# Retention's decayed queries made on GpSimd by token tile and transposed; group norm in two halves

## The chip, the core and the metric

The kernel runs on one core of one Trainium2 chip. The metric is device time in microseconds (us) of one execution; the median of several is given where there are several. One more execution of each kernel is profiled.

## What is computed

One layer of a diffusion backbone: a modulated RMS norm, one input projection, softmax attention (8 heads, 2 key heads, 64 wide) beside bidirectional retention (8 heads), one output projection, and a dense SwiGLU network. There are 1024 latent tokens and 256 context tokens, the width is 1024, all in float32. The change touches retention and its norm, which the reference gives as:

```python
q_decay = jnp.exp(lg[:, None] * (pos + 1.0))[..., None]
def step(state, qkv):
    qc, kc, vc = qkv
    inner = jnp.einsum('bhid,bhjd->bhij', qc, kc) * decay_mat
    o = jnp.einsum('bhij,bhjd->bhid', inner, vc) + jnp.einsum('bhid,bhde->bhie', qc, state) * q_decay
    state = state * chunk_decay + jnp.einsum('bhjd,bhje->bhde', kc * k_decay, vc)
    return state, o
o = o_f + o_b[:, ::-1]
mu = jnp.mean(o, axis=-1, keepdims=True)
var = jnp.mean(jnp.square(o - mu), axis=-1, keepdims=True)
ret = (o - mu) * lax.rsqrt(var + EPS) * silu(g_r)
```

It is done over chunks of 128 tokens, once forward and once over the reversed sequence, each direction with its own decay per head.

## The kernel before

Everything is one function. After the projections (to about 357 us) comes a stage that weaves three streams, written as Python generators: `attention()` (four head pairs, two halves of the queries, ten key tiles; two scores with an exponential and one weighing per tile), `front(h)` for the coming heads (split, transposes, row maxima), and `retain(r)` for four head pairs `r`, one after the other. `weave` gives each stream a number of steps and always advances the one that is furthest behind; a `yield` ends a step. The planned counts are `N_FR, N_RT, N_AT = 13, 38, 40`. The build then orders each engine's instructions by a timeline that it simulates, so that an instruction may stand earlier on its engine than the program has it; `tc.issue_after(x)` keeps the instructions under it behind `x`. Every engine takes its queue in order, and a matmul that waits holds up all matmuls behind it.

A round of `retain(r)` goes through these steps:

- `ret_load` (L708) loads queries, keys, values and gate of the head pair, in tiles of 128 tokens (`rq`, `rk`, `rv`, `rg`), from the SP queue.
- Ten steps: `decayed(t)` (L737, GpSimd) multiplies a key tile by a decay per token, for two heads and two directions, into `qk2` (named `qk` in rows; three buffers); TensorE makes the state increments (L751), ScalarE copies them to `U` (L754, L756).
- In round 0 `decay_matrices` makes `DT` (L721 to L726), the decay matrix of each head, and `QD` (L730), the queries' decay by position for each head half and direction.
- Four steps: TensorE transposes keys and queries (L768, bank `r`), ScalarE copies them to `kT`, `qT` (L769). After each half of `qT` four products with `QD` (L774) give `q2T`, direction 0 on VectorE, direction 1 on GpSimd. Each takes 64 partitions with 512 elements and may move them to the other 64 partitions.
- The scan `ss` over the chunks (L782, VectorE, 16 dependent links of 128x64), copied to `St` (L787, L789, ScalarE).
- `inner(t)`: the products of `qT` and `kT` (L799), multiplied with `DT` by VectorE to `im` (L802). `outer(t)`: `im` with the values (L811) and `q2T` with `St` (L813) added up in PSUM, copied to `ro` (L815).
- Group norm of the whole head pair, 16 groups of 64 for each of 128 partitions: sum, subtraction (L834 to L836, VectorE), square (L839, ScalarE), sum (L840, L841, VectorE), the power on GpSimd (L843), the product with it on VectorE (L845), the product with the gate on GpSimd (L846), the store to `d_r` (L847).

Beside it attention adds up its exponentials in `acc` (L688), on GpSimd for half of the key tiles or more, and the fronts take row maxima `mx` from PSUM (L596, VectorE). The first transposes of a front are at L587, its query split at L577 and L578, its last transposes at L604 and L605. After the last round `rts.close()` frees retention's memory, and `load_w_out` loads and splits the output weights (L875, L125, L126) beside the last head pair of attention, whose results are normalised at L670. Then `mix_in` and `mix_out` begin.

```python
Q_ENG[d].tensor_tensor(out=q2T[d * HD:(d + 1) * HD, j, bsl].rearrange("p (t n) -> p t n", n=P),
                       in0=qT[jsl, bsl].rearrange("p (t n) -> p t n", n=P),
                       in1=QD[jsl, r, d, :].unsqueeze(1).broadcast_to([HD, 4, P]), op=ALU.mult)
```

Of the kernel before, what the change touches and what calls it, by code (L numbers as in the profile page):

```python
# [107 lines left out]
def hybrid_block(ctx: ExitStack, tc, x, c, cx, c_ctx, w_mod, b_mod, g_pre_mix, g_post_mix,  # L108
# [5 lines left out]
    def f(ap):  # L114
        return ap.bitcast(F32)

    def h3(ap):
        return ap.rearrange("p (h d) -> p h d", d=HD)
# [422 lines left out]
        V.tensor_copy(out=lgd[d * HD:(d + 1) * HD, :], in_=lg[d * HD:(d + 1) * HD, d * HR:(d + 1) * HR])  # L541
    S.activation(out=cd, in_=lgd, func=AF.Exp, scale=float(P))

    lgq = bc.tile([P, 4, 2], F32, name="lgq")
    for j in range(2):
        for d in range(2):
            V.tensor_copy(out=lgq[j * HD:(j + 1) * HD, :, d],
                          in_=lg[j * HD:(j + 1) * HD, d * HR:(d + 1) * HR].rearrange("p (r j) -> p r j", j=2)[:, :, j])

    rawp = ph1.enter_context(tc.tile_pool(name="rawp", bufs=4))  # L550
    wks = ExitStack()
    wk1 = wks.enter_context(tc.tile_pool(name="wk1", bufs=1))
# [4 lines left out]
    late.step(2)  # L557
    wks.close()

    qs2, fr = {}, {}  # L560

    def falloc(first, shape, dt, tag, bufs):
        if first == 1:
# [5 lines left out]
    def front(h):  # L569

        kv = h // 4
        if h % 2 == 0:
            qs2[h // 2] = falloc(h, [P, LT, P], F32, "qs", 1)
            nc.sync.dma_start(out=qs2[h // 2], in_=d_p[0:N_LAT, h * HD:(h + 2) * HD].rearrange("(t p) n -> p t n", p=P))
        q3 = falloc(h, [P, LT, 2 * HD + 2], F32R, "q3", 2)
        qs = qs2[h // 2][:, :, (h % 2) * HD:(h % 2 + 1) * HD]
        S.copy(out=q3[:, :, HD:2 * HD], in_=qs)  # L577
        V.tensor_tensor(out=q3[:, :, 0:HD], in0=qs, in1=f(q3[:, :, HD:2 * HD]), op=ALU.subtract)  # L578
# [12 lines left out]
        nm = small.tile([P, LT], F32, tag="nm", name="nm")  # L591
        for t in range(LT):
            for j, (k0, n) in enumerate(((0, 512), (512, 512), (1024, 256))):
                sb = sbank()
                T.matmul(sb[:, :n], lhsT=t1[:, t * P:(t + 1) * P], rhs=K1[:, kv, k0:k0 + n], start=True, stop=True)  # L595
                V.tensor_reduce(out=mx[:, t, j:j + 1], in_=sb[:, :n], axis=AX.X, op=ALU.max)  # L596
            yield
        V.tensor_reduce(out=nm, in_=mx[:, :, 0:3], axis=AX.X, op=ALU.max, negate=True)
        V.tensor_copy(out=q3[:, :, 2 * HD:2 * HD + 1], in_=nm.unsqueeze(2))
        yield  # L600
        for b in range(2):
            tb = sbank(F32R)
# [6 lines left out]
    SKEW, V_ADDS, V_END, Q_ENG = 4, (2, 4, 6, 8), (2, 4, 6, 7, 8, 9), (V, G)  # L609
    weave((project, 18), (chain(front(0), front(1)), 2 * N_FR))  # L610
    ph1.close()
    ps1.close()
# [101 lines left out]

    DT = rt.tile([P, HR, P], F32, name="DT")

    QD = rt.tile([P, 4, 2, P], F32, name="QD")

    def decay_matrices():
        for h in range(HR):  # L720
            V.tensor_scalar(out=DT[:, h, :], in0=dcs[:, C_DF:C_DF + P], scalar1=lg[:, h:h + 1], scalar2=None, op0=ALU.mult)  # L721
# [2 lines left out]
        for h in range(0, HR, 4):  # L724
            S.activation(out=DT[:, h:h + 4, :], in_=DT[:, h:h + 4, :], func=AF.Exp)
            G.tensor_tensor(out=DT[:, h:h + 4, :], in0=DT[:, h:h + 4, :],  # L726
                            in1=dcs[:, C_M:C_M + P].unsqueeze(1).broadcast_to([P, 4, P]), op=ALU.mult)
        for r in range(4):
            for d in range(2):
                S.activation(out=QD[:, r, d, :], in_=dcs[:, C_PR + d * P:C_PR + (d + 1) * P], func=AF.Exp, scale=lgq[:, r, d:d + 1])  # L730

    def retain(r):
        qn, kn, vn, gn = ret_load(r)

        def decayed(t):
            y = rt.tile([P, 2, 2, HD], F32, tag="qk2", name="qk2", bufs=3)
            G.tensor_tensor(out=y, in0=h3(kn[:, t, :]).unsqueeze(2).broadcast_to([P, 2, 2, HD]),  # L737
                            in1=dk[:, 1, 4 * r:4 * r + 4].rearrange("p (j d) -> p j d", d=2).unsqueeze(3).broadcast_to([P, 2, 2, HD]),
                            op=ALU.mult)
            return y  # L740

# [14 lines left out]
                S.copy(out=U[HD:P, LT + 1 - t], in_=h3(ub[HD:P, 0:P]))  # L756
            yield
        if r == 0:
            decay_matrices()
        qT = rt.tile([P, N_LAT], F32, tag="qT", name="qT")  # L760
        kT = rt.tile([P, N_LAT], F32, tag="kT", name="kT")
        q2T = rt.tile([P, 2, N_LAT], F32, tag="q2T", name="q2T")
        for nat, tr in ((kn, kT), (qn, qT)):
            for b in range(2):
                tb = bank("r")
                bsl = slice(b * 512, (b + 1) * 512)
                for i in range(4):
                    T.transpose(out=tb[:, i * P:(i + 1) * P], in_=nat[:, b * 4 + i, :], identity=ident)  # L768
                S.copy(out=tr[:, bsl], in_=tb)  # L769
                if nat is qn:  # L770
                    for j in range(2):
                        jsl = slice(j * HD, (j + 1) * HD)
                        for d in range(2):
                            Q_ENG[d].tensor_tensor(out=q2T[d * HD:(d + 1) * HD, j, bsl].rearrange("p (t n) -> p t n", n=P),  # L774
                                            in0=qT[jsl, bsl].rearrange("p (t n) -> p t n", n=P),
                                            in1=QD[jsl, r, d, :].unsqueeze(1).broadcast_to([HD, 4, P]), op=ALU.mult)
                yield

        ss = rt.tile([P, LT, 2, HD], F32, tag="ro", name="ss")
        for i in range(LT):  # L780
# [53 lines left out]
        V.tensor_reduce(out=mu, in_=o4, axis=AX.X, op=ALU.add)  # L834
        V.tensor_scalar(out=mu, in0=mu, scalar1=1.0 / HD, scalar2=None, op0=ALU.mult)
        V.tensor_tensor(out=o4, in0=o4, in1=mu.unsqueeze(2).broadcast_to([P, nst, HD]), op=ALU.subtract)  # L836
        yield
        sq = rt.tile([P, nst, HD], F32, tag="kT", name="gsq")
        S.activation(out=sq, in_=o4, func=AF.Square)  # L839
        V.tensor_reduce(out=vr, in_=sq, axis=AX.X, op=ALU.add)  # L840
        V.tensor_scalar(out=vr, in0=vr, scalar1=1.0 / HD, scalar2=EPS, op0=ALU.mult, op1=ALU.add)  # L841
        for k in range(2):
            G.tensor_tensor(out=rs[:, k * 8:(k + 1) * 8], in0=vr[:, k * 8:(k + 1) * 8], in1=mhalf, op=ALU.pow)  # L843
        yield
        V.tensor_tensor(out=o4, in0=o4, in1=rs.unsqueeze(2).broadcast_to([P, nst, HD]), op=ALU.mult)  # L845
        G.tensor_tensor(out=gn, in0=o.rearrange("p t j e -> p t (j e)"), in1=gn, op=ALU.mult)  # L846
# [435 lines left out]
```

## Time and profile before

| | us |
|---|---|
| median of 3 runs | 1534.27 |
| lowest, highest | 1531.69, 1535.69 |
| the profiled execution | 1534.52 |
| its span | 1532.7 |
| TensorE matmuls busy | 1447.2 |
| VectorE busy | 866.4 |
| ScalarE busy | 518.6 |
| GpSimd busy | 501.7 |

In the rows PE is TensorE's matmuls, PEld its weight loads, DVE VectorE, ACT ScalarE, POOL GpSimd, SP the queue that issues the transfers. L774 is line 774 of the kernel. Matmuls are pipelined and their ends are modelled, so a busy PE need not be at its peak. PEclk is the granted clock of TensorE as a share of 2.4 GHz; it has two levels, 2.4 and 1.2 GHz, and a share between is a mean over the time. What ended a wait is inferred from semaphore events.

### The profile page before, as it was taken

The numbers are of one execution on the slowest core, as the hardware profiler recorded it, in microseconds if no ns is written. First come the engines' busy times: TensorE is split into PE (matmuls) and PEld (weight loads), VectorE is DVE, ScalarE is ACT, GpSimd is POOL, SyncE is SP. The second block draws the span as 40 slices with busy tenths as digits, with TensorE's granted clock in tenths as the row PEclk, the third lists the DMA queues.
The fourth block names the chain that finished last, engine by engine and source line by source line (L and its number), as shares of the span: only waits on it lengthen the run. The fifth ranks groups of instructions, "written<-read, shape, count | busy, mean of one in ns | idle before, by whom it ended". The sixth has DMA issues, their size and how long they took to land.

```text
span 1532.7 us, 19765 instructions
## 1 busy us (share of the span) xinstructions
PE 1447.2 (94%) x7290; PEld 1083.8 (71%) x7290; DVE 866.4 (57%) x1447; ACT 518.6 (34%) x1131; POOL 501.7 (33%) x382
## 2 busy tenths in 40 slices
PE   6999989998898989799899899999999999999997
PEld 2788867785454545454588678888888888888886
DVE  3667677445747676676455845444444444545445
ACT  3740221224344444545245623222222232113112
POOL 0112247303435273545003544444444441002003
PEclk9999999998676989899899999999999999999999
DMA  9456552314102020002433233222222224544662
GB/s 357 137 187 189 184 168 90 114 52 126 31 25 73 25 66 25 28 8 97 134 132 120 62 97 96 83 83 83 83 83 83 83 83 152 178 145 134 197 211 109
DMA packets 140623, 169.10 MB, mean 110 GB/s; under 512 B 8992, under 2 KB 90608, under 8 KB 140528
## 3 DMA queue, kind: packets, MB, share of 16 engines
q1 hardware_dynamic: 139680, 167.61, 33.9%
q8 instruction: 57, 0.93, 0.3%
q10 hardware_dynamic: 848, 0.25, 0.1%
q14 instruction: 38, 0.31, 0.1%
HBM read 132.17 MB, written 35.65 MB: 109 GB/s over the span
## 4 chain that ended last, share of the span: by engine, by line
PE 76%; DVE 11%; DMA 6%; issue 2%; ACT 2%; POOL 2%; SPq 0%; DVEq 0%; POOLq 0%; ACTq 0%
PE pb L131 45%; PE sb L131 14%; PE o L640 4%; PE sb L631 3%; PE sb L595 2%; DMA wm<-in_w_mod 2%; PE sb L632 2%; DVE q2T L774 1%; DMA rv<-d_p 1%; PE r L799 1%; DVE ss L782 1%; DVE mx L596 1%; PE sb L811 1%; PE r L751 1%; DVE wlo L126 1%
## 5 line engine op out<-in xcount | busy, mean ns | idle before, releaser
L131 PE MATMUL pb<-T,w 128*128 128x512 f32 x1320 | 316.7, 394 | 3.8 <-ACT w L125 2.0
L131 PEld LDWEIGHTS pb<-T,w 128*128 128x128 f32 x1320 | 247.8, 188 | 62.6 <-ACT w L125 2.6
L131 PE MATMUL pb<-whi,hT 128*128 128x512 f32 (+1 forms) x896 | 261.8, 373 | 5.2 <-ACT whi L125 4.6
L131 PEld LDWEIGHTS pb<-whi,hT 128*128 128x128 f32 x896 | 162.7, 191 | 39.3 <-ACT whi L125 5.5
L131 PE MATMUL pb<-wlo,hT 128*128 128x512 f32 (+1 forms) x448 | 165.7, 372 | 2.3 <-DVE wlo L126 2.2
L596 DVE TENSOR_REDUCE mx<-sb 128x1 f32<-128x512 f32 (+1 forms) x192 | 107.0, 596 | 62.9 <-PE sb L595 61.5
L126 DVE TENSOR_TENSOR w<-w1raw,w 128x512 fp32r<-128x512 f32 x152 | 123.3, 868 | 12.6 <-ACT w L125 12.6
L131 PE MATMUL sb<-B,w 128*128 128x512 f32 x504 | 124.8, 391 | 0.8 <-ACT u L1059 0.8
L633 ACT ACTIVATE p<-sb 128x512 f32<-128x512 f32 x160 | 92.3, 598 | 81.0 <-PE sb L632 77.0
L125 ACT CAST w<-w1raw 128x512 fp32r<-128x512 f32 x152 | 83.7, 619 | 94.1 <-POOL w1raw L1006 92.4
L688 POOL TENSOR_TENSOR acc<-acc,p 128x1024 f32<-128x1024 f32 x30 | 71.3, 2376 | 119.7 <-ACT p L633 109.1
L131 PEld LDWEIGHTS sb<-B,w 128*128 128x128 f32 x504 | 94.4, 188 | 22.1 <-ACT u L1059 1.3
L1138 POOL TENSOR_TENSOR g<-g,c 128x512 f32<-128x512 f32 x22 | 34.4, 1565 | 215.0 <-DVE c L1137 190.0
L131 PE MATMUL pb<-w,ah 128*128 128x512 f32 x328 | 101.5, 389 | 0.0
L640 PE MATMUL o<-p,VV 128*64 128x512 f32 x320 | 98.9, 684 | 2.8 <-ACT p L633 2.7
L131 PE MATMUL sb<-w,ah 128*128 128x512 f32 x328 | 101.4, 389 | 0.0
L131 PEld LDWEIGHTS pb<-wlo,hT 128*128 128x128 f32 x448 | 85.5, 191 | 18.7 <-DVE wlo L126 3.4
L176 POOL TENSOR_TENSOR ss<-ss,mhalf 128x1 f32<-128x1 f32 x26 | 14.7, 571 | 243.4 <-DVE ss L175 243.4
L131 PE MATMUL pb<-woh,rT 128*128 128x512 f32 x256 | 82.1, 401 | 0.6 <-DVE rT L125 0.6
L125 ACT CAST w<-raw 128x512 fp32r<-128x512 f32 x41 | 25.4, 624 | 168.5 <-PE pb L131 152.4
L125 DVE CAST ah<-ra 128x1024 fp32r<-128x1024 f32 x41 | 28.6, 698 | 88.4 <-PE pb L131 88.4
L631 PE MATMUL sb<-t,K 128*128 128x512 f32 x140 | 70.6, 504 | 7.7 <-DVE mx L596 5.8
(258 smaller groups left out, 2471.2 us busy)
## 6 DMA issues: line engine op xcount, KB each, us to landing
w1raw<-in_w_ffn_in SPq DMA_DIRECT2D x92, 256.0 KB, 3.4
ra<-d_a SPq DMA_DIRECT2D x41, 512.0 KB, 4.2
wm<-in_w_mod SPq DMA_DIRECT2D x64, 256.0 KB, 3.5
raw<-in_w_ffn_out SPq DMA_DIRECT2D x41, 256.0 KB, 3.9
d_p<-st SPq DMA_DIRECT2D x34, 256.0 KB, 2.0
wm<-in_w_mod SPq DMA_DIRECT2D x16, 512.0 KB, 6.8
raw<-in_w_in SPq DMA_DIRECT2D x32, 256.0 KB, 4.5
d_a<-g SPq DMA_DIRECT2D x22, 256.0 KB, 2.0
```

The lines of the kernel that those rows point to most:

```text
L125: a = S.copy(out=hi, in_=src) if hi_eng is S else hi_eng.tensor_copy(out=hi, in_=src)
L126: return a, V.tensor_tensor(out=lo, in0=src, in1=f(hi), op=ALU.subtract)
L131: T.matmul(acc, lhsT=a, rhs=b, start=first and a is ah and b is bh, stop=last and a is al, skip_group_check=onto)
L595: T.matmul(sb[:, :n], lhsT=t1[:, t * P:(t + 1) * P], rhs=K1[:, kv, k0:k0 + n], start=True, stop=True)
L596: V.tensor_reduce(out=mx[:, t, j:j + 1], in_=sb[:, :n], axis=AX.X, op=ALU.max)
L631: T.matmul(sb, lhsT=K1[:, h // 4, ksl], rhs=t1[:, qsl], start=True, stop=False)
L632: T.matmul(sb, lhsT=K2[:, h // 4, ksl], rhs=t2[:, qsl], start=False, stop=True)
L633: S.activation(out=p[:, :, h % 2, :], in_=sb.rearrange("p (i n) -> p i n", n=P), func=AF.Exp)
L640: return T.matmul(st["o"][j * HD:(j + 1) * HD, :], lhsT=VV[kt][:, r // 2, :], rhs=p[:, :, j, :], start=(kt == 0), stop=(kt == AT - 1))
L688: eng.tensor_tensor(out=st["a"], in0=prev if kt == 1 else st["a"], in1=p, op=ALU.add)
L751: T.matmul(ub[d * HD:(d + 1) * HD, j * HD:(j + 1) * HD], lhsT=k2[t][:, j, d, :], rhs=vn[:, t, j * HD:(j + 1) * HD], start=True, stop=True)
L1138: G.tensor_tensor(out=g0, in0=g0, in1=c21, op=ALU.mult)
```

## The change

`QD` and its `lgq` go. The queries are decayed as the keys are, by `decayed` on GpSimd (`src=qn, w=0`), one token tile of 128x256 at a time; TensorE transposes the result, four 128x128 for two tiles, and ScalarE copies it to `q2T`. The `qk2` ring grows from three to four buffers. `decay_matrices` is put behind the query split of the last front that has begun. Group norm is done by halves of the token tiles, each on its own step. A round has 49 steps in place of 39, and the plan `N_RT` is 47. The scan, `inner`, `outer` and all else stay.

```diff
-        for r in range(4):
-            for d in range(2):
-                S.activation(out=QD[:, r, d, :], in_=dcs[:, C_PR + d * P:C_PR + (d + 1) * P], func=AF.Exp, scale=lgq[:, r, d:d + 1])
...
-        def decayed(t):
-            y = rt.tile([P, 2, 2, HD], F32, tag="qk2", name="qk2", bufs=3)
-            G.tensor_tensor(out=y, in0=h3(kn[:, t, :]).unsqueeze(2).broadcast_to([P, 2, 2, HD]),
-                            in1=dk[:, 1, 4 * r:4 * r + 4].rearrange("p (j d) -> p j d", d=2).unsqueeze(3).broadcast_to([P, 2, 2, HD]),
+        def decayed(t, src=kn, w=1):
+
+            y = rt.tile([P, 2, 2, HD], F32, tag="qk2", name="qk2", bufs=4)
+            G.tensor_tensor(out=y, in0=h3(src[:, t, :]).unsqueeze(2).broadcast_to([P, 2, 2, HD]),
+                            in1=dk[:, w, 4 * r:4 * r + 4].rearrange("p (j d) -> p j d", d=2).unsqueeze(3).broadcast_to([P, 2, 2, HD]),
                             op=ALU.mult)
...
         if r == 0:
-            decay_matrices()
+            with tc.issue_after(hold["q"].ins):
+                decay_matrices()
...
                 S.copy(out=tr[:, bsl], in_=tb)
-                if nat is qn:
-                    for j in range(2):
-                        jsl = slice(j * HD, (j + 1) * HD)
-                        for d in range(2):
-                            Q_ENG[d].tensor_tensor(out=q2T[d * HD:(d + 1) * HD, j, bsl].rearrange("p (t n) -> p t n", n=P),
-                                            in0=qT[jsl, bsl].rearrange("p (t n) -> p t n", n=P),
-                                            in1=QD[jsl, r, d, :].unsqueeze(1).broadcast_to([HD, 4, P]), op=ALU.mult)
+                if nat is qn and b:
+                    q2 = [decayed(t, qn, 0) for t in range(2)]
                 yield
+
+        for t in range(0, LT, 2):
+            cur, q2 = q2, [decayed(t + 2 + i, qn, 0) for i in range(2)] if t + 2 < LT else None
+            tb = bank("r")
+            for i in range(2):
+                for j in range(2):
+                    T.transpose(out=tb[:, (2 * i + j) * P:(2 * i + j + 1) * P], in_=cur[i][:, j].rearrange("p d f -> p (d f)"),
+                                identity=ident)
+            S.copy(out=q2T[:, :, t * P:(t + 2) * P].rearrange("p j (i n) -> p i j n", n=P),
+                   in_=tb.rearrange("p (i j n) -> p i j n", i=2, n=P))
+            yield
...
+        halves = [slice(0, LT), slice(LT, nst)]
+        for h in halves:
+            V.tensor_reduce(out=mu[:, h], in_=o4[:, h], axis=AX.X, op=ALU.add)
+            yield
...
+        for h in halves:
+            V.tensor_tensor(out=o4[:, h], in0=o4[:, h], in1=mu[:, h].unsqueeze(2).broadcast_to([P, LT, HD]), op=ALU.subtract)
+            S.activation(out=sq[:, h], in_=o4[:, h], func=AF.Square)
+            yield
+        for h in halves:
+            V.tensor_reduce(out=vr[:, h], in_=sq[:, h], axis=AX.X, op=ALU.add)
+            V.tensor_scalar(out=vr[:, h], in0=vr[:, h], scalar1=1.0 / HD, scalar2=EPS, op0=ALU.mult, op1=ALU.add)
+            G.tensor_tensor(out=rs[:, h], in0=vr[:, h], in1=mhalf, op=ALU.pow)
+            yield
+        for h in halves:
+            V.tensor_tensor(out=o4[:, h], in0=o4[:, h], in1=rs[:, h].unsqueeze(2).broadcast_to([P, LT, HD]), op=ALU.mult)
+            G.tensor_tensor(out=gh[:, h], in0=oh[:, h], in1=gh[:, h], op=ALU.mult)
+            yield
...
-    N_FR, N_RT, N_AT = 13, 38, 40
+    N_FR, N_RT, N_AT = 13, 47, 40
```

## Rows read from the trace of the kernel before

**Rows 1.** Page of the kernel before: busy totals, and granted clock of 40 slices of 38.3 us

```profile
PE 1447.2 (94%) x7290; PEld 1083.8 (71%) x7290; DVE 866.4 (57%) x1447; ACT 518.6 (34%) x1131; POOL 501.7 (33%) x382
...
PEclk9999999998676989899899999999999999999999
```

**Rows 2.** Busy time (instructions) by stretch: PE, PEld, DVE, ACT, POOL, granted clock, DMA

```profile
390.00:440.00 50.00, 45.44 (x193) 22.99 (x192) 22.71 (x46) 15.01 (x31) 16.25 (x11) 0.59 0.06 18
...
470.00:510.00 40.00, 34.17 (x165) 18.25 (x164) 22.77 (x48) 14.09 (x30) 16.20 (x11) 0.66 0.18 53
...
510.00:550.00 40.00, 39.90 (x340) 23.06 (x339) 27.83 (x45) 21.83 (x50) 22.00 (x14) 1.00 0.09 27
...
560.00:580.00 20.00, 13.07 (x54) 6.62 (x53) 16.80 (x26) 4.49 (x9) 9.58 (x8) 0.74 0.04 12
...
620.00:650.00 30.00, 22.15 (x116) 12.15 (x115) 20.69 (x33) 13.62 (x28) 16.28 (x9) 0.77 0.12 36
```

**Rows 3.** Timeline of the second round: start, us, engine, line, wait before in brackets

```profile
466.73 7.54 DVE L774 TENSOR_TENSOR q2T<-qT,QD 64x512 f32<-64x512 f32 x4
...
470.43 3.28 POOL L774 TENSOR_TENSOR q2T<-qT,QD 64x512 f32<-64x512 f32 x2
...
474.30 0.29 DVE L802 TENSOR_TENSOR im<-r,DT 128x128 f32<-128x128 f32 x1
...
474.64 0.37 PEld L799 LDWEIGHTS r<-qT,kT 64*128 64x128 f32 x2 [3.76 <-DVE im L802]
```

**Rows 4.** Instructions on `q2T`: least, median and most ns

```profile
L774 POOL TENSOR_TENSOR q2T<-qT,QD x16: 1261/1610/2262, 390.1 to 631.3; 64x512 f32<-64x512 f32 x16
L774 DVE TENSOR_TENSOR q2T<-qT,QD x16: 675/1661/2766, 391.6 to 630.2; 64x512 f32<-64x512 f32 x16
```

**Rows 5.** The chain of waits, 340 to 760 us, by line

```profile
by line: PE o L640 14.0%; PE sb L631 9.8%; PE sb L595 7.3%; PE pb L131 6.8%; PE sb L632 6.6%; DVE q2T L774 5.1%; DMA rv<-d_p 4.3%; PE r L799 4.2%; DVE ss L782 3.9%; DVE mx L596 3.7%; PE sb L811 3.1%; PE r L751 2.9%; DMA raw<-in_w_out 2.8%; 
```

**Rows 6.** Instructions on `qk`: least, median and most ns

```profile
L737 POOL TENSOR_TENSOR qk<-rk,dk x40: 602/612/1596, 365.5 to 615.2; 128x256 f32<-128x256 f32 x40
```

**Rows 7.** Groups of 360 to 740 us: busy us, mean ns, idle before and releasers

```profile
L737 POOL TENSOR_TENSOR qk<-rk,dk 128x256 f32<-128x256 f32 x40 | 30.0, 773 | 92.8 <-DMA rk<-d_p 78.2 <-PE r L751 14.0 <-DVE vr L840 0.4
...
L688 POOL TENSOR_TENSOR acc<-acc,p 128x1024 f32<-128x1024 f32 x30 | 71.3, 2376 | 119.7 <-ACT p L633 109.1 <-DVE acc L688 5.1 <-issue 3.8
...
L782 DVE SCALAR_TENSOR_TENSOR ss<-ss,cd,U 128x64 f32<-128x64 f32 x56 | 22.3, 447 | 0.1
...
L751 PEld LDWEIGHTS r<-rv,qk 128*64 128x64 f32 x320 | 13.2, 141 | 13.9 <-issue 6.6 <-POOL qk L737 3.4 <-DMA rv<-d_p 2.5
...
L768 PE MATMUL r<-ident,rq 128*128 128x128 f32 x32 | 4.8, 277 | 0.0
...
L769 ACT COPY qT<-r 128x512 f32<-128x512 f32 x8 | 4.6, 586 | 2.9 <-PE r L768 2.9
...
L730 ACT ACTIVATE QD<-dcs,lgq 128x128 f32<-128x128 f32 x8 | 2.7, 396 | 1.5 <-DMA dcs<-in_dec 1.5
...
L722 DVE SCALAR_TENSOR_TENSOR DT<-dcs,lg,DT 128x128 f32<-128x128 f32 x8 | 2.4, 347 | 0.0
...
L721 DVE TENSOR_SCALAR DT<-dcs,lg 128x128 f32<-128x128 f32 x8 | 1.8, 282 | 1.5 <-DMA dcs<-in_dec 1.5
```

**Rows 8.** Timeline of the head of the stage

```profile
364.27 1.29 DVE L578 TENSOR_TENSOR q<-qs,q 128x512 fp32r<-128x512 f32 x2 [0.68 <-ACT q L577]
...
365.17 0.72 PE L587 MATMUL sb<-identr,q 128*128 128x128 f32 x4 [2.85 <-issue]
...
373.42 0.69 DVE L596 TENSOR_REDUCE mx<-sb 128x1 f32<-128x512 f32 x1 [7.86 <-PE sb L595]
```

**Rows 9.** Timeline of the last round's norm and the end of the stage

```profile
677.57 1.22 DVE L834 TENSOR_REDUCE mu<-ro 128x16 f32<-128x1024 f32 x1
...
738.28 0.69 DVE L126 TENSOR_TENSOR wol<-raw,woh 128x512 fp32r<-128x512 f32 x1 [1.51 <-ACT woh L125]
...
739.59 0.69 DVE L670 TENSOR_TENSOR oh<-sb,oh 128x512 f32<-128x512 f32 x1 [0.62 <-PE sb L668]
```

More of the change, by code (lines that the diff above doesn't have):

```diff
@@ L542, in hybrid_block @@
     S.activation(out=cd, in_=lgd, func=AF.Exp, scale=float(P))
-    lgq = bc.tile([P, 4, 2], F32, name="lgq")
-    for j in range(2):
-        for d in range(2):
-            V.tensor_copy(out=lgq[j * HD:(j + 1) * HD, :, d],
-                          in_=lg[j * HD:(j + 1) * HD, d * HR:(d + 1) * HR].rearrange("p (r j) -> p r j", j=2)[:, :, j])
     rawp = ph1.enter_context(tc.tile_pool(name="rawp", bufs=4))
@@ L558, in hybrid_block @@
     wks.close()
-    qs2, fr = {}, {}
+    qs2, fr, hold = {}, {}, {}
     def falloc(first, shape, dt, tag, bufs):
@@ L577, in front @@
         S.copy(out=q3[:, :, HD:2 * HD], in_=qs)
-        V.tensor_tensor(out=q3[:, :, 0:HD], in0=qs, in1=f(q3[:, :, HD:2 * HD]), op=ALU.subtract)
+        hold["q"] = V.tensor_tensor(out=q3[:, :, 0:HD], in0=qs, in1=f(q3[:, :, HD:2 * HD]), op=ALU.subtract)
         yield
@@ L608, in hybrid_block @@
     N_FR = 15
-    SKEW, V_ADDS, V_END, Q_ENG = 4, (2, 4, 6, 8), (2, 4, 6, 7, 8, 9), (V, G)
+    SKEW, V_ADDS, V_END = 4, (2, 4, 6, 8), (2, 4, 6, 7, 8, 9)
     weave((project, 18), (chain(front(0), front(1)), 2 * N_FR))
@@ L715, in hybrid_block @@
     DT = rt.tile([P, HR, P], F32, name="DT")
-    QD = rt.tile([P, 4, 2, P], F32, name="QD")
     def decay_matrices():
@@ L769, in retain @@
                 S.copy(out=tr[:, bsl], in_=tb)
-                if nat is qn:
-                    for j in range(2):
-                        jsl = slice(j * HD, (j + 1) * HD)
-                        for d in range(2):
-                            Q_ENG[d].tensor_tensor(out=q2T[d * HD:(d + 1) * HD, j, bsl].rearrange("p (t n) -> p t n", n=P),
-                                            in0=qT[jsl, bsl].rearrange("p (t n) -> p t n", n=P),
-                                            in1=QD[jsl, r, d, :].unsqueeze(1).broadcast_to([HD, 4, P]), op=ALU.mult)
-                yield
+                if nat is qn and b:
+                    q2 = [decayed(t, qn, 0) for t in range(2)]
+                yield
+        for t in range(0, LT, 2):
[8 more added lines that the diff above has]
+            yield
         ss = rt.tile([P, LT, 2, HD], F32, tag="ro", name="ss")
@@ L833, in retain @@
         rs = rt.tile([P, nst], F32, tag="rsg", name="rsg")
-        V.tensor_reduce(out=mu, in_=o4, axis=AX.X, op=ALU.add)
+        halves = [slice(0, LT), slice(LT, nst)]
+        oh, gh = o.rearrange("p t j e -> p (t j) e"), gn.rearrange("p t (j e) -> p (t j) e", e=HD)
+        for h in halves:
+            V.tensor_reduce(out=mu[:, h], in_=o4[:, h], axis=AX.X, op=ALU.add)
+            yield
         V.tensor_scalar(out=mu, in0=mu, scalar1=1.0 / HD, scalar2=None, op0=ALU.mult)
-        V.tensor_tensor(out=o4, in0=o4, in1=mu.unsqueeze(2).broadcast_to([P, nst, HD]), op=ALU.subtract)
-        yield
         sq = rt.tile([P, nst, HD], F32, tag="kT", name="gsq")
[L839 to L846, printed above, removed]
+        for h in halves:
[11 more added lines that the diff above has]
+            yield
         nc.sync.dma_start(out=d_r[:, r * P:(r + 1) * P].rearrange("(t p) n -> p t n", p=P), in_=gn)
         yield
-    N_FR, N_RT, N_AT = 13, 38, 40
+    N_FR, N_RT, N_AT = 13, 47, 40
     attend = attention()
```

## Prediction, before the run

> **What bounds the kernel now.** I read the page's totals first. TensorE is busy for 94% of the span, so a gain has to come from its losses, and the row of the granted clock shows where they are thickest: it falls to 6 and 7 tenths in three of the 40 slices only, from 383 to 498 us, with single slices of 8 around them [rows 1]. That is the stage in which attention, the next heads' fronts and four rounds of retention (one per head pair) are woven together.
>
> Next I cut the stage into stretches. Four of them stand out against the undisturbed stretch at 510 us, where TensorE is busy for 39.90 of 40 us at full clock with 340 matmuls [rows 2]. In the four, TensorE is idle for 4.56, 5.83, 6.93 and 7.85 us, 25.2 in all, and the clock is 0.59, 0.66, 0.74 and 0.77: a mix of the two levels, 1.2 and 2.4 GHz, after each idle time. Busy time times one minus clock gives 18.6 + 11.6 + 3.4 + 5.1 = 38.7 us that the same matmuls would not have needed at 2.4 GHz. The stalls thus cost 63.9 us, more in the clock behind them than in themselves. As a check, the four stretches do 528 matmuls in 140 us, which at the undisturbed rate of 8.5 per us would take 62: a loss of 78, of the same size (the mix of matmuls differs).
>
> There is one stretch per round, and each has the `q2T` products in it. The timeline of the second shows why TensorE stops: VectorE is in four products for 7.54 us, GpSimd's run beside them, and a matmul of L799 waits 3.76 us for an `im` which VectorE reaches only at 474.30 [rows 3]. The products go slowly because they run together: on VectorE the same form takes 675 ns at least and 1661 in the median [rows 4]. The chain of waits over 340 to 760 us confirms it: `q2T` on VectorE has 5.1% of the stretch, the scan `ss` 3.9%, the row maxima 3.7% [rows 5].
>
> **The change, part by part.**
>
> *VectorE's products go.* 16 products of 1661 ns in the median, 26.6 us of VectorE [rows 4], stand on the chain. They share the four stalls with the scan, which stays. I split the loss by the chain's shares: 5.1 / (5.1 + 3.9) = 57%, so 0.57 x 63.9 = 36.4 us are gained. The bounds are 0 (the scan and the maxima would hold TensorE as long) and 63.9 (nothing is left). I take the share, since the chain is the row nearest to what ends a wait.
>
> *GpSimd's products go, 32 decays come.* GpSimd loses 16 x 1.610 = 25.8 us [rows 4] and gains 32 of the kind that it does for `k` (128x256, L737): 19.6 us at their median of 0.612 [rows 6], 24.7 at their mean of 0.773 [rows 7]. I take the median, since what lengthens the mean is mostly VectorE's work beside them, of which less is left; at either value GpSimd does not get busier. The products of 64x512 took GpSimd 1261 ns at least and VectorE 675, a factor of 1.87 [rows 4], but the new form uses all 128 partitions: a round's 8 decays, 4.9 us, do what both engines did, and GpSimd's half alone took 6.4. The Trainium skill, GPSIMD Engine Reference (its opening, and Performance versus the Vector engine), speaks against such a move: GpSimd is the wrong choice for ordinary elementwise arithmetic, with VectorE about twice as fast. By that rule GpSimd would take an estimated 21.6 us for what VectorE can do in 10.8, and the time would come out as in the first rival; by the rows the sum stays as it is.
>
> *Transposes come.* 64 more on TensorE. A group of 32 of such takes 4.8 us, 0.15 each (L768) [rows 7]: 9.6 us, all on the path since TensorE is the bound. Bounds: 0 if they fall into waits, 19.2 at half clock. I take 9.6, the row's own value.
>
> *Copies on ScalarE.* 16 of 128x512 at 0.586 (L769) come, 9.4 us; the 8 `QD` exponentials at 0.396 go, 3.2 us [rows 7]. Net 6.2 us on an engine that is busy 22 of 40 us even in the undisturbed stretch [rows 2]: I count nothing, 6.2 without that cover.
>
> *The head of the stage.* `QD` is gone and `DT` waits for the front's query split. Until now ScalarE's `QD` and VectorE's `DT` (1.8 + 2.4 us) [rows 7] ran ahead of that split, which VectorE starts at 364.27, so TensorE's transposes came at 365.17 [rows 8]. I take 2 us, bounds 0 and 2.7 (`QD`'s own busy time). Queued behind the delayed `DT` on VectorE are the first maxima; VectorE idles 7.86 us before these [rows 8], which hides 4.2 us. `DT` itself is not needed before the first `im`, some 30 us on.
>
> *Group norm in halves.* A norm step of 128x1024 takes 1.22 us [rows 9]; two halves can be bounded by the split's two of 128x512 (1.29) [rows 8], so the 16 steps of 128x1024 in four rounds cost 0 to 1.1 us more, and let maxima in between. Behind the last round's norm comes the loading of `w_out`; its last split starts at 738.28, but the last normalisation of attention only at 739.59 [rows 9], so what the norm saves at the end is hidden by attention's own end. I count 0, bounds -4 and +1.1.
>
> *Queues and order.* No DMA is added. On SP the next round's load of `rq` must now wait for the last decay of `q` instead of the last transpose into `qT`: a few us, with the loads and stores of `rg` behind it, all wanted a round later, so nothing. Cover gone, it would be the length of the four steps, about 6 us once a round. On GpSimd the decays queue behind additions into `acc` (2.376 us) [rows 7], and TensorE's transposes wait for them with all scores behind them; that is the first rival. The step counts go from 39 to 49 a round and the planned 38 to 47, so that a round still spans 31 attention steps.
>
> Sum: -36.4 - 2 + 9.6 = -28.8 us. The profiled execution took 1534.52 (span 1532.7), 0.25 above the median of three: 1534.5 - 28.8 = **1505.7**.
>
> **Rivals.**
>
> *TensorE waits for GpSimd (slower).* Place: the 16 steps with new transposes. Price: a step's pair of decays is 1.2 us; behind an addition of 2.4 it is 3.6. From 365.17 to 677.57 us [rows 8, 9] the four rounds' 196 steps leave about 1.6 us each as cover, so a hit step costs 2.0 us. All 16 hit: 32 us idle, and at the present ratio of clock loss to idle (38.7 to 25.2) another 49: -28.8 + 81 = +52, 1587. It decides from about 6 hit steps (6 x 5.1 = 30 us). For it: GpSimd is busy 16 of 40 us in such stretches [rows 2] and must also do the norm's power and product. Against: the 40 steps over `k` have the same shape, one decay ahead, and TensorE's loads waited only 3.4 us for them [rows 7]. With 8 steps hit: 1546.
>
> *The clock stays low.* Stalls shrink by 57%, but the scan's remainder still drops the clock each time: -14.4 - 2 + 9.6 = -6.8, 1527.7. For it: the clock fell in all four stretches, whether TensorE's idle time in them was 4.56 us or 7.85 [rows 2], so a shorter stall may not spare it. Against: the 0.10 us of idle time in the undisturbed stretch left it at 1.00.
>
> *The scan runs free as well.* Its links take 447 ns in the mean [rows 7], and some of that is time beside GpSimd's long products. If nothing is left of the stalls: -63.9 - 2 + 9.6 = -56.3, 1478.2.
>
> *It doesn't do what it says.* If scan and maxima hold TensorE nearly as long, and the share is 15% and not 57%, the gain equals the transposes: 1534 within 4.
>
> **How the numbers follow.** A measurement here can tell about 0.3%, 4.6 us. Forecast 0.53 (1492 to 1520), free scan 0.12, low clock 0.15, no change 0.07, GpSimd 0.13. Faster: 0.53 + 0.12 + 0.15 = 0.80; same 0.07; slower 0.13. The range leaves out the GpSimd case and the tails: 1476 to 1535.
>
> **What would show it.** Right: L774 is gone, the four stretches lose less than 30 us in idle and clock together, `im`'s hold on L799 falls, and TensorE's new transposes wait for GpSimd for under 5 us. Wrong: transposes waiting for GpSimd by more than 10 us, clock stretches as long as before, or the scan's links as slow with TensorE behind them.

## The result, and the profile after

The changed kernel takes 1496.86 us in the median of four runs (1491.15 to 1498.97), the kernel before 1534.98 in the same comparison: a ratio of 0.9753, 95% interval 0.9731 to 0.9775, or 38 us less (34 to 41). The profiled execution took 1498.97 us. In the experiments below one slow run with the old products and one with the decays on VectorE, each over 1.5% above the fastest of its kernel, are left out of the medians. Lines of the changed file are others than before; L770 are the new transposes, L779 is the scan, L727 the decays of keys and queries, L590 the row maxima, L625 and L626 the scores, L796 the `inner` products.

First the page of the changed kernel: span, busy totals, granted clock. It answers to [rows 1].

```profile
span 1497.2 us, 19980 instructions
...
PE 1430.2 (96%) x7354; PEld 1077.7 (72%) x7354; DVE 851.6 (57%) x1447; ACT 525.1 (35%) x1143; POOL 495.7 (33%) x402
...
PEclk8999999999999999879999899999999999999999
```

The three slices at 6 and 7 tenths are gone. Apart from the first of all, what is left below 9 are the slices of 599 to 674 us (8 and 7), in the last round and behind it, and one of 8 near 840 us, outside the stage. TensorE is now busy for 96% of a shorter span, though it does 64 matmuls more.

Then the stage as a whole, from the first state increment to the last `inner` product. These two instructions bound the four rounds in both kernels, and the rows below are the busy time of each engine in just this stretch (columns as in [rows 2]): the kernel before, then the changed one.

```profile
367.00:670.00 303.00, 274.54 (x1852) 154.98 (x1852) 196.53 (x345) 134.24 (x305) 141.73 (x94) 0.84 0.14 42
```

```profile
369.00:631.00 262.00, 248.94 (x1922) 145.37 (x1922) 185.94 (x353) 141.91 (x324) 136.40 (x113) 0.97 0.17 48
...
390.00:440.00 50.00, 48.17 (x400) 28.52 (x399) 30.81 (x69) 29.22 (x66) 23.89 (x21) 1.00 0.14 42
...
640.00:665.00 25.00, 22.34 (x94) 11.54 (x94) 11.51 (x16) 10.93 (x20) 12.62 (x8) 0.66 0.10 32
```

The rounds are 41 us shorter (303 to 262). TensorE's idle time in them falls from 28.5 to 13.1 us, and the clock rises from 0.84 to 0.97, so that busy time times one minus clock falls from 43.9 to 7.5 us. Idle and clock together lose 51.8 us. Against that stand 10.9 us more work at full clock (274.54 x 0.84 = 230.6 before, 248.94 x 0.97 = 241.5 after). 51.8 - 10.9 = 40.9, as it must be, since the three parts make up the time; with the clock read to two digits each part is uncertain by 1 to 3 us. The old first stretch is a good place to see it: [rows 2] had 193 matmuls in 390 to 440 us at a clock of 0.59, and now there are 400 at 1.00. The last row shows what remains. After the last `inner`, 640 to 665 us, VectorE is in the norm of the last round, a front's transposes wait 2.79 us for the copy of its maxima, and the clock is 0.66.

By instructions: from the first increment to the last `inner` 301.3 us before and 260.8 after; from there to the first transpose of the output projection's stage 72.7 and 75.3; from there to the end 790.9 and 791.6. All of the gain lies in the rounds, and 36.7 us of it in the first two (their starts are 83.3 and 82.8 us apart before, 58.8 and 70.6 after), where the clock had been low the longest.

The chain of waits over the stage (340 to 720 us), answering to [rows 5], and the groups of instructions that answer to [rows 7] (busy us, mean ns, idle before and releasers). The last fence is the kernel before, where the loads of the `inner` products are at L799.

```profile
by line: PE o L634 13.4%; PE sb L625 9.6%; PE sb L589 7.7%; PE pb L131 7.0%; PE sb L626 6.3%; DVE ss L779 5.6%; DMA raw<-in_w_out 5.2%; PE r L796 4.8%; DVE mx L590 3.6%; PE sb L808 3.2%; DVE wol L126 2.8%; PE r L741 2.6%; DMA rv<-d_p 2.5%; 
```

```profile
L779 DVE SCALAR_TENSOR_TENSOR ss<-ss,cd,U 128x64 f32<-128x64 f32 x56 | 22.6, 452 | 0.0
...
L727 POOL TENSOR_TENSOR qk<-rq,dk 128x256 f32<-128x256 f32 x32 | 21.0, 680 | 10.1 <-PE r L770 10.1
...
L796 PEld LDWEIGHTS r<-qT,kT 64*128 64x128 f32 x128 | 14.7, 188 | 18.9 <-issue 8.5 <-DVE im L799 2.6 <-DVE acc L682 2.4
...
L770 PE MATMUL r<-ident,qk 128*128 128x128 f32 x64 | 11.3, 291 | 0.0
...
L770 PEld LDWEIGHTS r<-ident,qk 128*128 128x128 f32 x64 | 8.0, 147 | 6.8 <-issue 3.4 <-POOL qk L727 2.3
```

```profile
L799 PEld LDWEIGHTS r<-qT,kT 64*128 64x128 f32 x128 | 18.0, 224 | 35.7 <-DVE im L802 14.8 <-issue 12.4 <-DVE mx L596 3.0
```

`q2T` has left the chain and the scan has 5.6% of it where it had 3.9. The scan's links are no faster (452 ns in the mean, 447 before). The loads of the `inner` products waited 14.8 us for `im` and now wait 2.6. The loads of scores and fronts waited 12.3 and 9.9 us for the maxima (L631 and L595 of the kernel before) and now wait 6.1 and 6.7. The loads of the new transposes wait 2.3 us for GpSimd's decays, five times. The decays themselves take 21.0 us of GpSimd where its products took 25.8.

The head of the stage, as a timeline (start, us, engine, line, idle time before in brackets): the kernel before, then the changed one. L422 is the last copy of the projections in both.

```profile
356.65 0.38 ACT L422 ACTIVATE st<-pb 128x256 f32<-128x256 f32 x1 [3.41 <-PE pb L131]
...
357.05 1.28 ACT L730 ACT_TABLE_LOAD   x1
```

```profile
358.48 0.38 ACT L422 ACTIVATE st<-pb 128x256 f32<-128x256 f32 x1 [3.40 <-PE pb L131]
...
361.73 1.28 ACT L627 ACT_TABLE_LOAD   x1
...
365.55 0.69 DVE L572 TENSOR_TENSOR q<-qs,q 128x512 fp32r<-128x512 f32 x1 [5.45 <-ACT q L571]
```

The stage begins 1.8 us later, because the projections ended later. From L422 to the query split on VectorE it is 7.6 us before (364.27 in [rows 8]) and 7.1 after. With `QD` gone the table load of ScalarE no longer runs ahead, while `QD` waits for its data; it now stands before the first score's exponential.

### The profile page after: what moved, and what is told of

It is laid out like the page before. It is cut to its first block, busy times and chain, and to the rows that moved or that the text cites. A ratio compares the mean times of both kernels' runs of the same rounds, so it can differ in the third digit from the quotient of the medians.

```text
span 1497.2 us, 19980 instructions
## 1 busy us (share of the span) xinstructions
PE 1430.2 (96%) x7354; PEld 1077.7 (72%) x7354; DVE 851.6 (57%) x1447; ACT 525.1 (35%) x1143; POOL 495.7 (33%) x402
## 4 chain that ended last, share of the span: by engine, by line
PE 79%; DVE 8%; DMA 6%; ACT 3%; issue 2%; POOL 2%; SPq 0%; DVEq 0%; ACTq 0%; POOLq 0%
PE pb L131 48%; PE sb L131 15%; PE o L634 3%; PE sb L625 2%; PE sb L589 2%; DMA wm<-in_w_mod 2%; PE sb L626 2%; DVE ss L779 1%; DMA raw<-in_w_out 1%; PE r L796 1%; DVE mx L590 1%; PE sb L808 1%; DVE wol L126 1%; DMA raw<-in_w_in 1%; PE r L741 1%
## 5 line engine op out<-in xcount | busy, mean ns | idle before, releaser
L131 PE MATMUL pb<-whi,hT 128*128 128x512 f32 (+1 forms) x896 | 264.9, 377 | 4.4 <-ACT whi L125 3.7
L590 DVE TENSOR_REDUCE mx<-sb 128x1 f32<-128x512 f32 (+1 forms) x192 | 107.0, 594 | 48.8 <-PE sb L589 47.9
L627 ACT ACTIVATE p<-sb 128x512 f32<-128x512 f32 x160 | 92.7, 599 | 70.1 <-PE sb L626 69.1
L131 PEld LDWEIGHTS sb<-B,w 128*128 128x128 f32 x504 | 94.4, 188 | 22.2 <-ACT u L1063 1.2
L634 PE MATMUL o<-p,VV 128*64 128x512 f32 x320 | 92.0, 655 | 4.7 <-ACT p L627 4.6
L625 PE MATMUL sb<-t,K 128*128 128x512 f32 x140 | 67.7, 484 | 4.8 <-DVE oh L664 1.6
```

Source lines behind the costliest of these rows:

```text
L131: T.matmul(acc, lhsT=a, rhs=b, start=first and a is ah and b is bh, stop=last and a is al, skip_group_check=onto)
L625: T.matmul(sb, lhsT=K1[:, h // 4, ksl], rhs=t1[:, qsl], start=True, stop=False)
L627: S.activation(out=p[:, :, h % 2, :], in_=sb.rearrange("p (i n) -> p i n", n=P), func=AF.Exp)
L634: return T.matmul(st["o"][j * HD:(j + 1) * HD, :], lhsT=VV[kt][:, r // 2, :], rhs=p[:, :, j, :], start=(kt == 0), stop=(kt == AT - 1))
```

## The experiments

All times are medians; each ratio is to the kernel before on the same chip, and the experiments ran on three chips. The changed kernel's own ratio is 0.9753 (0.9731 to 0.9775). A difference of two medians and a difference of two ratios can lie 4 to 6 us apart, so small differences are told both ways.

### The old products back

`QD`, its table and `Q_ENG = (V, G)` come back as they were, and the four steps with transposes go. The ring has three buffers again; the halves of the norm and the hold stay, and the plan has its own count of steps:

```diff
-                if nat is qn and b:
-                    q2 = [decayed(t, qn, 0) for t in range(2)]
+                if nat is qn:
+                    for j in range(2):
+                        jsl = slice(j * HD, (j + 1) * HD)
+                        for d in range(2):
+                            Q_ENG[d].tensor_tensor(out=q2T[d * HD:(d + 1) * HD, j, bsl].rearrange("p (t n) -> p t n", n=P),
+                                            in0=qT[jsl, bsl].rearrange("p (t n) -> p t n", n=P),
+                                            in1=QD[jsl, r, d, :].unsqueeze(1).broadcast_to([HD, 4, P]), op=ALU.mult)
...
-    N_FR, N_RT, N_AT = 13, 47, 40
+    N_FR, N_RT, N_AT = 13, 43, 40
```

> The changed kernel with the 64x512 products and their table back (three buffers in the ring), but with the norm in halves and the decay matrices held back. If the products on VectorE beside those on GpSimd are what cost the time, as the prediction has it, this falls back to 1525 to 1537 us and shows four stretches with a lowered clock again. If the norm in halves brings a good part, it stays under 1515 us.

Measured: 1522.70 us, ratio 0.9929 (0.9897 to 0.9961). Groups of the stage, busy time over its four rounds, and over 35 us behind the first round's products, with the last 28 of them by themselves; then the same 35 us in the kernel before:

```profile
L777 DVE TENSOR_TENSOR q2T<-qT,QD 64x512 f32<-64x512 f32 x16 | 22.0, 1376 | 0.1
...
L802 PEld LDWEIGHTS r<-qT,kT 64*128 64x128 f32 x128 | 18.2, 208 | 33.8 <-DVE im L805 17.5 <-issue 10.5 <-DVE mx L596 2.1
```

```profile
366.00:655.00 289.00, 260.48 (x1849) 148.19 (x1851) 199.09 (x371) 135.09 (x308) 140.45 (x95) 0.89 0.15 44
...
402.00:437.00 35.00, 34.29 (x297) 19.64 (x296) 15.69 (x39) 17.28 (x37) 10.72 (x7) 0.91 0.09 28
409.00:437.00 28.00, 27.29 (x258) 16.16 (x256) 13.45 (x31) 14.22 (x31) 8.37 (x6) 1.00 0.11 35
```

```profile
402.00:437.00 35.00, 35.00 (x144) 17.40 (x143) 10.22 (x24) 11.30 (x22) 7.04 (x3) 0.50 0.00 1
```

Most of the loss is back. The loads of the `inner` products wait 17.5 us for `im` again, and idle time and clock cost 28.5 + 28.7 = 57.2 us of the 289. It is 2 us under the range that my theory gave, and 11 us (6 to 16) better than the kernel before, so something in the rest of the change helps while the products are there. It does not help by fewer stops: TensorE idles 28.5 us in the rounds in both kernels, and the waits for `im` are no shorter (17.5 us, 14.8 before). What differs is the clock behind them, 28.7 us in place of 43.9. The last rows show the largest piece of that: behind the first round's products the kernel before stays at the lower level, 1.2 GHz, for these 35 us, with TensorE busy all the time, while in this run the clock is at 1.00 from 409 us on. The hold alone, further below, says one thing that it is not.

### The norm in whole

```diff
-        for h in halves:
-            V.tensor_reduce(out=mu[:, h], in_=o4[:, h], axis=AX.X, op=ALU.add)
...
+        V.tensor_reduce(out=mu, in_=o4, axis=AX.X, op=ALU.add)
...
-    N_FR, N_RT, N_AT = 13, 47, 40
+    N_FR, N_RT, N_AT = 13, 41, 40
```

> The changed kernel with the group norm of before, in whole. The prediction gave the norm nothing (bounds -4 and +1.1 us): 1493 to 1501 us. If the norm's long VectorE instructions were part of the stall, 1505 to 1515 us.

Measured: 1495.71 us, ratio 0.9765 (0.9724 to 0.9806). Beside the new queries the halves bring nothing that can be told.

### Without the hold

```diff
-            with tc.issue_after(hold["q"].ins):
-                decay_matrices()
+            decay_matrices()
```

> The changed kernel without the hold that puts the decay matrices behind the front's query split. The prediction gave table and hold 2 us together, so about 1499 us, at most 1500. In the trace of the changed kernel the first state increments come 1.7 us later than before, so the rival is that the hold brings nothing or costs: 1495 to 1497 us.

Measured: 1495.21 us, ratio 0.9757 (0.9703 to 0.9812). The hold brings nothing here either; the two expectations lie nearer to each other than this run can tell apart, but it leans to the rival.

### The hold alone

This is an edit of the kernel before:

```diff
-            decay_matrices()
+            with tc.issue_after(hold["q"].ins):
+                decay_matrices()
```

> The kernel before with nothing but the hold: decay matrices and the products' table come behind the front's query split. In the run with the old products the first round took 66 us against 83 before, and the norm comes only after it. If the hold made that, this takes 1517 to 1526 us; if it was the norm in halves or the new plan of steps, or chance, 1530 to 1537 us.

Measured: 1532.87 us, ratio 0.9996 (0.9970 to 1.0022). So it was not the hold by itself that made the 11 us of the first experiment. Left for it are the norm in halves and the new plan of steps, which no run took apart. In the first round, the largest piece, the clock had returned by 409 us in the run with the old products and the first sum of the norm starts only at 415.56, which speaks for the plan; it is not shown. With the products gone, halves and hold bring nothing that can be told; the old plan was not run with the new queries, and the fourth buffer of the ring has no run of its own.

### Transposes twice, and four times

```diff
-            for i in range(2):
+            for i in (0, 0, 0, 0, 1, 1, 1, 1):
                 for j in range(2):
                     T.transpose(out=tb[:, (2 * i + j) * P:(2 * i + j + 1) * P], in_=cur[i][:, j].rearrange("p d f -> p (d f)"),
```

The diff is that of the second run; the first has each twice.

> The changed kernel with each of the 64 new transposes done twice into the same place. By the prediction's term of 0.15 us each it is 9.6 us slower, 1506.5 us. If the transposes fall into time in which TensorE would wait anyway, the cost is 0 to 4 us and the term was too high.

> The changed kernel with each of the 64 new transposes done four times into the same place, 192 more. At the prediction's 0.15 us each this is 28.8 us slower, about 1526 us. Doing them twice cost 2.5 us by the medians; if most of them fall into time in which TensorE waits, four times cost 12 us at most, 1509 us or less.

Measured: twice 1499.41 us, ratio 0.9793 (0.9748 to 0.9838); four times 1507.92 us, ratio 0.9853 (0.9813 to 0.9893). Twice costs 2.5 us by the medians and 6 by the ratios, between the two expectations by the latter. The 192 transposes more cost 11 us by the medians and 15 by the ratios, 0.058 to 0.08 us each: at the rival's upper end or somewhat over it, and far from 28.8. The busy time of the four rounds in the run with four times, and the group:

```profile
369.00:640.00 271.00, 264.42 (x2088) 163.24 (x2090) 180.68 (x350) 140.88 (x320) 133.17 (x111) 0.99 0.15 44
```

```profile
L770 PE MATMUL r<-ident,qk 128*128 128x128 f32 x256 | 31.5, 274 | 0.0
```

They do work: 264.42 x 0.99 = 261.8 us at full clock against 241.5, 20 us more, 0.11 each. But the rounds are only 9 us longer by these windows, since idle time (6.6 us) and clock (2.6) now cost 9.2 in place of 20.6. In these two executions about half of the added work went into time that TensorE lost before, part of it in the clock.

### All products on VectorE, all on GpSimd

Two edits of the kernel before; the second has `(G, G)` in the same place:

```diff
-    SKEW, V_ADDS, V_END, Q_ENG = 4, (2, 4, 6, 8), (2, 4, 6, 7, 8, 9), (V, G)
+    SKEW, V_ADDS, V_END, Q_ENG = 4, (2, 4, 6, 8), (2, 4, 6, 7, 8, 9), (V, V)
```

> The kernel before with all 32 products on VectorE and none on GpSimd. VectorE then does 32 of 0.675 us, 21.6 us, where it was held for 26.6. If the two engines holding each other up is what made the stall, it is no slower than before: 1525 to 1535 us. If it is the amount of work that VectorE has in front of the row maxima, it is slower: 1538 to 1548 us.

> The kernel before with all 32 products on GpSimd and none on VectorE: 32 of 1.26 us or more, 40 us, a round 10 us. If freeing VectorE is what counts, most of the gain is here without any transposes: 1495 to 1512 us. If GpSimd then becomes what the state products on TensorE wait for, or holds up the scan on VectorE for as long as the products did, 1530 us or more.

Measured: all on VectorE 1529.26 us, ratio 0.9970 (0.9937 to 1.0003); all on GpSimd 1511.30 us, ratio 0.9867 (0.9829 to 0.9904). The groups of the stage, first all on VectorE, then all on GpSimd:

```profile
L774 DVE TENSOR_TENSOR q2T<-qT,QD 64x512 f32<-64x512 f32 x32 | 29.8, 930 | 0.4
...
L782 DVE SCALAR_TENSOR_TENSOR ss<-ss,cd,U 128x64 f32<-128x64 f32 x56 | 18.1, 374 | 0.1
```

```profile
L774 POOL TENSOR_TENSOR q2T<-qT,QD 64x512 f32<-64x512 f32 x32 | 44.9, 1405 | 6.2 <-ACT qT L769 4.6
...
L782 DVE SCALAR_TENSOR_TENSOR ss<-ss,cd,U 128x64 f32<-128x64 f32 x56 | 37.7, 726 | 0.0
...
L799 PEld LDWEIGHTS r<-qT,kT 64*128 64x128 f32 x128 | 14.0, 192 | 25.2 <-DVE im L802 12.8 <-issue 8.4 <-DVE mx L596 1.2
```

All on VectorE lies in the range that I had given to the pairing. Twice as many products take VectorE 29.8 us where half of them had taken 25.7, 689 ns in the median against 1661: alone, most of them are not held, so the pairing is what had made them long. But with products and scan together VectorE is taken for as long as before (47.9 us, 48.0 before), `inner`'s loads wait 12.4 us for `im`, and the time is the same: undoing the pairing brings nothing to speak of while the work stays on VectorE. With VectorE free of products, and no transpose added, about 20 of the 38 us are there (15 to 26). What is left in that run stands with the scan: its links take 726 ns in the mean, against 452 in the changed kernel, and `inner`'s loads still wait 12.8 us for `im`. The state products wait 3.1 us for GpSimd, so that part of the second expectation does not show.

### The decays on VectorE, and on ScalarE

```diff
-            G.tensor_tensor(out=y, in0=h3(src[:, t, :]).unsqueeze(2).broadcast_to([P, 2, 2, HD]),
+            (V if w == 0 else G).tensor_tensor(out=y, in0=h3(src[:, t, :]).unsqueeze(2).broadcast_to([P, 2, 2, HD]),
```

```diff
+            if w == 0:
+                for j in range(2):
+                    for d in range(2):
+                        cc = 4 * r + 2 * j + d
+                        S.activation(out=y[:, j, d, :], in_=src[:, t, j * HD:(j + 1) * HD], func=AF.Identity,
+                                     scale=dk[:, w, cc:cc + 1])
```

> The changed kernel with the decayed queries made on VectorE in place of GpSimd, 32 instructions of 128x256, about 0.41 us each by the rotary products of that size, 13 us. If the form (128 partitions, no pairing) is what counts, within 4 us of the changed kernel, 1493 to 1501 us. If it counts that VectorE is free of this work, 5 to 13 us slower, 1502 to 1510 us.

> The changed kernel with the decayed queries made on ScalarE, four instructions of 128x64 with a scale per token for each tile, 128 in all, in place of 32 on GpSimd. If GpSimd's decays still hold up the scan on VectorE (its links take 496 ns in the mean, where the least is 266), this is 3 to 10 us faster, 1487 to 1494 us. If ScalarE's exponentials come later for it, 1500 to 1510 us.

Measured: on VectorE 1504.41 us (1500.91 to 1514.05), ratio 0.9834 (0.9775 to 0.9894); on ScalarE 1510.75 us, ratio 0.9884 (0.9840 to 0.9929). The decays on VectorE (least, median, most ns), and the groups with ScalarE:

```profile
L727 DVE TENSOR_TENSOR qk<-rq,dk x32: 404/412/2587, 379.5 to 605.8; 128x256 f32<-128x256 f32 x32
```

```profile
L735 ACT ACTIVATE qk<-rq,dk 128x64 f32<-128x64 f32 x128 | 34.2, 338 | 0.5
...
L786 DVE SCALAR_TENSOR_TENSOR ss<-ss,cd,U 128x64 f32<-128x64 f32 x56 | 18.4, 373 | 0.0
...
L777 PEld LDWEIGHTS r<-ident,qk 128*128 128x128 f32 x64 | 7.9, 140 | 7.8 <-ACT q2T L779 3.0 <-ACT qk L735 2.7 <-ACT qT L767 0.8
...
L803 PEld LDWEIGHTS r<-qT,kT 64*128 64x128 f32 x128 | 17.5, 212 | 23.1 <-issue 11.4 <-ACT q2T L779 4.2 <-DVE mx L590 1.9
```

Both are slower than the decays on GpSimd, on VectorE by 8 us by the medians and 12 by the ratios. On VectorE one takes 412 ns in the median, on GpSimd 610, and still GpSimd is the place for it. The decays on VectorE are themselves held beside GpSimd, for up to 2587 ns. That VectorE's own time is what costs is argued: the profile of this run is of its fastest execution, and its loads of `inner` wait 3.9 us for `im` against 2.6. On ScalarE the scan gains as I thought (373 ns a link), but 34.2 us more work on that engine makes the copies late: transposes and `inner` products now wait for ScalarE's `q2T`. The time is just above the second range.

### The copy of the maxima on ScalarE

```diff
-        V.tensor_copy(out=q3[:, :, 2 * HD:2 * HD + 1], in_=nm.unsqueeze(2))
+        S.copy(out=q3[:, :, 2 * HD:2 * HD + 1], in_=nm.unsqueeze(2))
```

> The changed kernel with the copy of the row maxima into the query tile moved from VectorE to ScalarE. TensorE's transposes behind it waited 5.9 us in six fronts, because the copy stood behind GpSimd's work. If these waits are on the path, and the low clock after them, it is 4 to 12 us faster, 1485 to 1493 us. If something else is late next, 1496 to 1500 us.

Measured: 1494.74 us, ratio 0.9747 (0.9700 to 0.9794), not to be told from the changed kernel; it lies between the two ranges. Groups:

```profile
L593 ACT CAST q<-nm 128x8 fp32r<-128x8 f32 x6 | 1.2, 205 | 1.7 <-DVE nm L592 1.6
...
L598 PE MATMUL sb<-identr,q 128*65 128x128 f32 x48 | 4.7, 229 | 2.7 <-ACT q L593 2.7
```

The copy takes 205 ns and no longer waits, but the transposes still wait 2.7 us for it, where they had waited 5.9. A wait of 3 us less in six fronts is not what sets the end.

### The scan left out

```diff
-        for i in range(LT):
-            for j in range(2):
-                V.scalar_tensor_tensor(out=ss[:, i, j, :], in0=ss[:, i - 1, j, :] if i else U[:, 0, j, :],
-                                       scalar=cd[:, 2 * r + j:2 * r + j + 1], in1=U[:, i + 1, j, :], op0=ALU.mult, op1=ALU.add)
+        V.tensor_copy(out=ss, in_=U[:, 1:])
```

> The changed kernel without the scan: its 16 dependent links a round are replaced by one copy of the state increments, so the states are not summed up over the chunks. The prediction left 43% of the stalls to the scan, and its rival had 1478 us if nothing were left. If the scan holds what remains, 1475 to 1487 us; if the rest belongs to other waits, 1491 to 1498 us.

Measured: 1479.99 us, ratio 0.9669 (0.9637 to 0.9701). Busy time of its four rounds, from the first increment to the last `inner`:

```profile
368.00:617.00 249.00, 243.34 (x1902) 142.93 (x1902) 163.88 (x290) 138.23 (x322) 136.15 (x111) 0.99 0.16 49
```

17 us less than the changed kernel by the medians, 13 by the ratios, within the range that the scan had. The rounds are 13 us shorter. Idle time and clock cost 5.7 + 2.4 us in them, where they cost 20.6 in the changed kernel, so some 12 us, more than half of what is left of the stalls, hang on the scan; the other 8 do not.

## Why the prediction was right, and where its sizes were off

The forecast was 1505.7 us with a likeliest range of 1492 to 1520; 1496.86 lies in it. Direction and mechanism held: the products stood in the way of `im` and of the maxima (the waits for both are down, from 14.8 to 2.6 us and from 22.2 to 12.8), TensorE stopped, and the clock fell behind these stops.

*VectorE's products: 36.4 us forecast, 51.8 measured* in idle time and clock over the rounds, for the change as a whole. The step that was mis-sized is the split by the chain's shares, 57% of 63.9. It treats the scan and the products as two parts that add up. They did not: the scan's links stayed as slow, and yet 51.8 of the 72.4 us that the rounds had lost are gone. A share of a chain says who was last at each moment, not what would be left if one went. What the products cost also depends on what stands beside them: put back into the changed kernel they cost 57.2 - 20.6 = 36.6 us, the forecast's figure, and the other 15.2 are the clock that the rest of the change had won already in that run, though halves and hold win nothing once the products are gone. So it is partly luck that the forecast's figure comes back there. The rival that nothing is left was wrong by the scan, which still costs 13 to 17 us; its time of 1478.2 is near what the run without the scan took (1479.99), but that run still loses 8 us in its rounds, so this too is in part luck.

*GpSimd: no busier, and not waited for.* 21.0 us against the 19.6 forecast. The loads of the new transposes waited 2.3 us for it, under the 5 that I had named, so the rival that ended slower fell. The rule of the Trainium skill, GPSIMD Engine Reference (its opening), that VectorE is the faster place for such work agrees with the durations here, 610 ns against 412; for the kernel the measurement decides the other way, since it is slower with the decays on VectorE.

*Transposes: 9.6 us forecast.* As busy time that was right: the rounds do 10.9 us more at full clock. As a cost it was too high: by the run with four times as many, each adds 0.058 to 0.08 us and not 0.15. By that an estimate for the first 64 is 4 to 5 us; no run took them away. I counted TensorE as the bound in a stage in which it idled for 13 us and lost 7.5 to the clock.

*ScalarE's copies: nothing forecast.* Scores' exponentials wait no longer than before (70.1 us of idle time before them, 81.0 in the kernel before), but the cover is not wide: 34.2 us of decays there cost 14 us by the medians, 20 by the ratios.

*Head: 2 us forecast, about 0.* From the last projection copy to the query split 0.5 us are gained, and the whole stage starts 1.8 us later. *Norm: 0 forecast, 0 found* beside the new queries. At the end of the stage 2.6 us were lost from the last `inner` to the output projection, in the low clock of 640 to 665 us.

*The clock* was the larger part of the gain, as the working had it: 43.9 - 7.5 = 36.4 of the 51.8 us (the forecast's 36.4 is the same figure by chance). The working let the clock's part shrink in step with the idle time. It does not: behind the first round's products the clock was low for 35 us and more in the kernel before, and for under 12 in the run with the old products put back. The rival that it stays low would have needed a fall in every round; in the rounds it now falls once for long, near 600 us, and for a moment near 455.

## What to carry to other kernels

Before moving work between engines, ask which engine's queue the stopped matmul's operand stands in, and free that one, even at the price of a slower engine and of more matmuls: here GpSimd's 610 ns beat VectorE's 412, 1496.86 us against 1504.41. Count the granted clock behind a stall together with the stall; it was the larger half. And take a share of the chain of waits as a rough guide only to what goes when one of two neighbours leaves: here 57% was forecast and 51.8 of 72.4 us, 72%, went.

## What the runs showed of the hardware

Some VectorE instructions stand still until a GpSimd instruction beside them ends, and others do not. A stretch of the second round in the changed kernel, as a timeline:

```profile
441.08 3.51 POOL L849 TENSOR_TENSOR rg<-ro,rg 128x512 f32<-128x512 f32 x2
...
443.37 1.61 DVE L590 TENSOR_REDUCE mx<-sb 128x1 f32<-128x512 f32 x3
...
446.33 2.93 DVE L779 SCALAR_TENSOR_TENSOR ss<-ss,cd,U 128x64 f32<-128x64 f32 x2
...
446.84 2.35 POOL L682 TENSOR_TENSOR acc<-acc,p 128x1024 f32<-128x1024 f32 x1
...
458.12 2.35 POOL L682 TENSOR_TENSOR acc<-acc,p 128x1024 f32<-128x1024 f32 x1 [0.18 <-ACT p L627]
...
458.35 2.15 DVE L593 CAST q<-nm 128x8 fp32r<-128x8 f32 x1
```

The whole trace of the changed kernel by instructions (least, median and most ns):

```profile
L779 DVE SCALAR_TENSOR_TENSOR ss<-ss,cd,U x56: 266/274/2389, 389.6 to 595.9; 128x64 f32<-128x64 f32 x56
...
L799 DVE TENSOR_TENSOR im<-r,DT x64: 276/282/292, 398.8 to 631.5; 128x128 f32<-128x128 f32 x64
...
L843 DVE TENSOR_REDUCE vr<-gsq x8: 672/678/689, 427.2 to 643.3; 128x8 f32<-128x512 f32 x8
```

Two scan links take 2.93 us and end as GpSimd's addition ends; a copy of 128x8, which takes 0.17 us when alone, takes 2.15 beside one. The three maxima at 443.37 read PSUM, lie partly beside GpSimd's product and take the usual half microsecond each. Nor are the products to `im`, with one operand in PSUM, ever lengthened (292 ns at most), and not even the sums of the norm (`vr`), which read SBUF alone: six of the eight lie beside a GpSimd instruction, and the longest takes 689 ns. So it is not enough to ask whether an instruction reads SBUF.

The Trainium skill, SBUF — State Buffer (SBUF: two separate sides), has this as a port pair that VectorE and GpSimd take in turns for a whole instruction, VectorE among others when it has two SBUF inputs and GpSimd reads SBUF too. The scan's links, with two such inputs, agree.

The mean of a link differs between the runs: 373 ns with the decays on ScalarE, 374 with all products on VectorE, 452 with decays of 610 ns on GpSimd, 726 with products of 1.4 us on it. But the median hardly does (271 to 279 in these four), and the longest is 2.3 to 2.4 us in each of them, the length of an addition. The mean goes with how many of the 56 links lie beside a GpSimd instruction, by their starts and ends: 8, 3, 21 and 42 in these runs. Whether its length or the engine's total counts is not shown: in the kernel before, with products of 1.6 us on GpSimd, the mean is 447, and with the decays on VectorE, none of these on GpSimd, it is 464. The additions into `acc` are the longest that the links meet, and no run took them off GpSimd.

Two more things were a surprise. More matmuls can cost about half of their time: with 192 added transposes the clock of the rounds went from 0.97 to 0.99 and idle time from 13.1 to 6.6 us. And the clock can stay at the lower level under work without a gap: in the kernel before from 402 to 437 us, TensorE busy for 35.00 of 35 us and the clock at 0.50, while the run with the old products was back at 1.00 from 409. What brings it back sooner is open.
